# A two-layer decoder on one core: where the low weight parts of some chunks lie, how many banks a gate takes, and when the y branch's function is due

## The chip, the cores and the metric

The kernel runs on one core of a Trainium2 chip. The metric is the device time of one execution in microseconds (us). The kernel before took 1972.53 us, the median of three runs (1972.23 to 1976.43). A profile is one further execution, recorded by the hardware profiler.

## The reference, cut to what matters

One sequence of 256 positions with 2048 features goes through two layers, all in float32.

- Layer 0, recurrent block: `h = rms_norm(x)`, `y, xb = split(h @ w_in)` (2048 to 2 x 2048), a causal convolution over four positions on `xb`, then two block-diagonal gates (8 blocks of 256 x 256 each), `r = sigmoid(...)` and `i = sigmoid(...)`, a linear recurrence over the positions, and `x += (hs * gelu(y)) @ w_out`.
- Layer 1, attention: keys and values of 4 heads from `x`, queries of 32 heads, a sliding window of 128 with a sink, and `x += out @ w_o`.
- After each of them a feed-forward part: `x += (silu(gate) * up) @ w_out`, 2048 to 2 x 5632 and 5632 back to 2048.

```python
y_branch, x_branch = jnp.split(h @ w_in, 2, axis=-1)
xb = causal_depthwise_conv(x_branch, conv_w, conv_b)
hs = rg_lru(xb, w_rg, b_rg, w_ig, b_ig, lam)
return x + (hs * jax.nn.gelu(y_branch)) @ w_out
```

## The kernel before

**Split products.** TensorE multiplies in a float32 format that keeps fewer bits (float32r). So each number is split into a high part and a low part, and a product of two numbers becomes three: high by high, high by low, low by high. `split` (lines 359 to 369) makes the two parts of a chunk of weights: ScalarE (ACT) copies `raw` to `hi`, VectorE (DVE) subtracts to get `lo`.

**Chunks.** All weights stream from memory through four buffers, in chunks of 128 x 1024 floats (512 KB). Each chunk is a job, appended to `self.jobs` as a triple: where it comes from, the function that multiplies, and a third entry that says how it is split. `stream` (line 390) goes through the jobs: it loads the chunk four jobs ahead, splits the chunk three jobs ahead and calls the multiplying function of the current one. A chunk holds two blocks of 128 input features by 512 output features, so a plain job has 2 x 4 x 3 = 24 products of 128 x 128 by 128 x 256.

**Order of the products.** In `group` (line 420) a group of four output tiles goes through all chunks of its columns. In the first and middle chunks the 16 products with the high weights come first (`a` and `b`, with the inputs' high and low part), then the 8 with the low weights (`l`). In a group's last chunk the order goes by output tile. The weights are the side that is loaded into TensorE ahead of the product (still), the inputs stream through (moving). In `fast_group` (line 588) and in parts of the attention it is the other way round.

**Places.** `raw`, `hi` and `lo` are four tiles each, then come temporaries and 37 slots `s0` to `s36` of 1024 floats. Between `s6` and `s7` lies a tile `step` of 16 floats (line 105). The slots from `s7` on ("far") hold the inputs and mixed weights, `s0` to `s6` ("near") some of the mixed weights. `hi` and `lo` have 128 floats to spare, and `parts` (line 354) says where in them a chunk begins: at 0 for some kinds of chunk, at `STEP` = 32 floats for the others.

**Fast groups.** The first feed-forward product has 22 groups per layer. Groups 0 to 3 are plain ones that start before the norm is known (`start`). The even ones from 4 to 20 use a Strassen-like scheme with seven products for eight (`fast_group`, with `mix` for the weights), in seven of their eight chunks (`PAIRS`). Chunks 0 and 4 (`EVEN`) keep their mixed weights in far slots and multiply those first. The odd groups from 5 to 21 are direct ones, with weights at 0; in group 21 the last two chunks have their weights at 32 floats. The results of a fast group are transposed by `turn` (line 781), which is held back until `flush` in a later chunk.

**The recurrent block.** `ORDER` (line 54) is the order of its jobs: four x groups, four y groups of eight chunks, and eight gates of one chunk each, mostly in pairs ahead of a y group. A gate (`gates`, line 916) multiplies two input tiles by four blocks into four banks of PSUM, and four sigmoids of 128 x 256 take them out. A y group ends with four pulls (`scaled`), and its function (`y_group`, line 978: a square, a tanh, the product with the recurrence's result) is a background task that is first due six half chunks later. The results, the `z`, are the inputs of `lru_out`.

**What sets the order.** Banks are handed out from a queue: whoever frees a bank puts it at the end. Background tasks are generators; `run_bg` steps those that are due while a count of the two engines' work stays below a limit, and `yield n` puts a task off by `n` half chunks. Behind that a planner reorders the instructions of each engine by their readiness and their place in the program.

Of the kernel before, what the change touches and what calls it, by code (L numbers as in the profile page):

```python
# [49 lines left out]
class Trunk:  # L50
# [11 lines left out]
    DEBT = 2500.0  # L62
    STEP = 32
    PLAIN = 4
# [289 lines left out]
    def parts(self, i):  # L354

        o = 0 if self.jobs[i][2] is not None else self.STEP
        return (q[i % 4][:, o:o + 1024] for q in (self.hi, self.lo))

    def split(self, i):
        raw = self.raw[i % 4]  # L360
        hi, lo = self.parts(i)
        if self.jobs[i][2]:
            self.mix(i, raw, hi, lo)
            return
        n = 512 if i == 0 else 1024
        for c in range(0, 1024, n):
            q = slice(c, c + n)
            self.nc.scalar.activation(hi[:, q], raw[:, q], AF.Copy)  # L368
            self.nc.vector.tensor_tensor(lo[:, q], raw[:, q], hi[:, q].bitcast(F32), ALU.subtract)  # L369

    def mix(self, i, raw, hi, lo):

        act, tt = self.nc.scalar.activation, self.nc.vector.tensor_tensor
        d = self.double(F32, True)
        near = self.jobs[i][2] == 1
        mh, ml = self.double(near=near), self.double(near=near)
        two = lambda ap: ap.rearrange("p (a c) -> p a c", c=T)
        q = slice(T, 4 * T)
        act(hi[:, q], raw[:, q], AF.Copy)  # L379
        tt(two(d[:, 0:2 * T]), two(raw[:, T:3 * T]), raw[:, 0:T].unsqueeze(1).to_broadcast([P, 2, T]), ALU.subtract)  # L380
        tt(d[:, 2 * T:3 * T], raw[:, 2 * T:3 * T], d[:, 0:T], ALU.add)
        tt(d[:, 3 * T:4 * T], raw[:, 3 * T:4 * T], d[:, 2 * T:3 * T], ALU.subtract)  # L382
        act(mh[:, :], d[:, :], AF.Copy)  # L383
        tt(lo[:, q], raw[:, q], hi[:, q].bitcast(F32), ALU.subtract)  # L384
        self.mark = tt(ml[:, :], d[:, :], mh[:, :].bitcast(F32), ALU.subtract)  # L385
        self.free(d)
        self.mixed[i] = (mh, ml)
        self.dve += self.MORE
# [30 lines left out]

    def group(self, src, nk, xs, done, last=False, four=False, pre=None, base=0):  # L420

# [3 lines left out]
        for c in range(nk // 2):  # L425
            def mm(hi, lo, c=c):
# [18 lines left out]
                if c == nk // 2 - 1:  # L445
                    done(st["ps"])
            self.jobs.append((src(c), mm, 0 if c < base else None))

# [98 lines left out]
    def by_turns(self, w, xs, gains, r):  # L547
# [4 lines left out]
        def job(g, c):  # L552
            def mm(hi, lo):
# [16 lines left out]
                if c == last:  # L570
                    self.residual(g, ps, gains, r, part=g)
            self.jobs.append((w[g, c], mm, None))

# [5 lines left out]
    def project(self, w, nk, xs, gains, r, out=None, turns=False):  # L579
        if turns:  # L580
            self.by_turns(w, xs, gains, r)
        for g in range(2 * turns, 4):
            def done(ps, g=g):
                self.residual(g, ps, gains, r, out)
            self.group(lambda c, g=g: w[g, c], nk, xs, done, g == 3)


    def fast_group(self, src, xn, mx, g, done, final):
# [49 lines left out]
        for c in range(8):  # L638
            def mm(hi, lo, c=c):
# [5 lines left out]
                if c == 7:  # L645
                    done(st["ps"])
            self.jobs.append((src(c), mm, (c in self.PAIRS) + (c in self.EVEN)))

# [5 lines left out]
    def ffn(self, l, xs, r, gains, rn, col, out=None):  # L654
# [68 lines left out]
        for g in range(NH // 2):  # L723
# [72 lines left out]
            if g < self.PLAIN:  # L796
                self.group(src, ND, xs, start, g == self.PLAIN - 1, True)
            elif g in self.FAST:
                self.fast_group(src, xn, mx, g, joined, g == self.FAST[-1])
            else:  # L800
                end = g == self.FAST[-1] + 1
                self.group(src, ND, xn, direct, g == NH // 2 - 1, True, 6 if end else None, 6 if end else 8)
            if g == 0:
# [64 lines left out]
    def lru(self, gains, rn):  # L868
# [47 lines left out]
        def gates(n):  # L916

            def mm(hi, lo):
                x2 = [self.need(xb[2 * n + kt]) for kt in range(2)]
                ps = [self.bank() for _ in range(4)]  # L920
                for j in range(4):
                    if j == 2:
                        self.half_tick()
                    for kt in range(2):
                        c = ((j // 2) * 2 + kt) * 256 + (j % 2) * P
                        for high, q in ((1, 0), (1, T), (0, 0)):
                            nc.tensor.matmul(ps[j][:, 0:T], (hi if high else lo)[:, c:c + P], x2[kt][:, q:q + T],
                                             start=kt == 0 and high > q, stop=kt == 1 and not high)
                v = []
                for j in range(4):  # L930
                    o = self.slot(F32)
                    col = (C_BR, C_BI)[j // 2] + 2 * n + j % 2
                    self.a(o[:, 0:T], ps[j][:, 0:T], AF.Sigmoid, bias=par[:, col:col + 1])
                    self.free_bank(ps[j])
                    v.append(o)
                for kt in range(2):
                    self.free(x2[kt])
                both.extend([(2 * n, v[0], v[2]), (2 * n + 1, v[1], v[3])])
                if n % 2:
                    self.spawn(recur(list(both)))  # L940
                    both.clear()
            self.jobs.append((self.d["gate"][n], mm, None))

# [34 lines left out]
        def y_group(g):  # L978
            def done(ps):
# [6 lines left out]
                def task():  # L986
                    yield 6
                    th = []
# [38 lines left out]
    def kv(self, xs, r, gains):  # L1027
# [66 lines left out]
        for c in range(8):  # L1094
            def mm(hi, lo, c=c):
# [40 lines left out]
                if c == 7:  # L1136
                    done(ps)
            self.jobs.append((w[c], mm, None))

    def attn(self, xs, r, gains, rn):  # L1140
# [163 lines left out]
        def queries(g, c):  # L1304
            st = self.qst

            def mm(hi, lo):
# [15 lines left out]
                if c == 7:  # L1323
                    self.spawn(finish(g, st[g]))
            self.jobs.append((w[g, c], mm, 0))

# [102 lines left out]
```

## Time and profile before

| | |
|---|---|
| median of three runs | 1972.53 us |
| the profiled execution: time, span | 1969.53 us, 1967.4 us |
| TensorE busy, matmuls | 1961.1 us, 16752 |
| VectorE (DVE) busy | 1523.4 us |
| ScalarE (ACT) busy | 1128.6 us |
| read from memory | 376.06 MB |

The span goes from the first instruction to the last, the time of the execution has some 2 us more around it. A busy TensorE says only that some product was under way: products overlap, each is listed with some 277 ns, and the distance from one start to the next is what counts. A view by stretches gives the busy time and the number of matmuls that lie in a stretch; a timeline lists instructions in order of their start.

Rough places in the span: the recurrent block's x, y and gates to 209 us, `lru_out` to about 296 us, the first feed-forward part to 1010 us (its second product from about 755 us on), keys, values and attention to 1213 us with `w_o`'s first half, then its second half, and the second feed-forward part from about 1236 us to the end (its second product from about 1719 us on).

### The profile page before, as it was taken

How to read it: one execution, taken by the hardware profiler on the slowest of the kernel's cores; microseconds unless marked ns; L12 is line 12 of the kernel's file. 1: busy time of each engine (PE TensorE's matmuls, PEld its weight loads, DVE VectorE, ACT ScalarE, POOL GpSimd, SP SyncE). 2: the span in 40 equal slices, each digit the busy share in tenths (PEclk: the TensorE clock that was granted, in tenths of full speed). 3: DMA queues.
4: the chain of work that ended last, by engine and by line, in shares of the span. 5: the costliest groups of instructions: out<-in, count | busy, mean ns of one | idle time of the engine just before them, and what ended most of it. 6: DMA issues, size and time to landing. Idle time of an engine off the chain costs nothing.

```text
span 1967.4 us, 40634 instructions
## 1 busy us (share of the span) xinstructions
PE 1961.1 (100%) x16752; PEld 1933.4 (98%) x16752; DVE 1523.4 (77%) x2425; ACT 1128.6 (57%) x1620; POOL 0.2 (0%) x4
## 2 busy tenths in 40 slices
PE   9999999999999999999999999999999999999999
PEld 9999999999999999999998889999999999999999
DVE  7988868999999997544667777698999998954443
ACT  7798746555556565434556766565555555743332
POOL 0000000000000000000000000000000000000000
PEclk9999999999999999999999999999999999999999
DMA  8555665566655667555554335656556565666663
GB/s 282 182 187 182 221 216 193 187 201 212 209 199 193 206 203 245 184 186 189 185 181 158 121 129 178 212 192 204 202 195 205 194 216 198 233 207 204 204 204 128
DMA packets 107321, 384.98 MB, mean 196 GB/s; under 512 B 11904, under 2 KB 14080, under 8 KB 107136
## 3 DMA queue, kind: packets, MB, share of 16 engines
q1 hardware_dynamic: 106848, 381.99, 58.7%
q8 instruction: 131, 2.15, 0.4%
q10 hardware_dynamic: 288, 0.40, 0.1%
q14 instruction: 54, 0.44, 0.1%
HBM read 376.06 MB, written 6.29 MB: 194 GB/s over the span
## 4 chain that ended last, share of the span: by engine, by line
PE 97%; DVE 1%; ACT 1%; issue 0%; DVEq 0%; ACTq 0%
PE b L416 67%; PE b L595 18%; PE b L1316 5%; PE b L567 2%; PE b L1167 1%; DVE lo L369 1%; PE b L1231 1%; PE b L1212 1%; PE b L1122 1%; ACT s L134 0%; DVE s L147 0%; PE b L785 0%; ACT hi L368 0%; PE b L1290 0%; PE b L1356 0%
## 5 line engine op out<-in xcount | busy, mean ns | idle before, releaser
L416 PE MATMUL b<-s,hi 128*128 128x256 f32 x7936 | 1026.6, 277 | 1.3 <-ACT s L134 1.3
L416 PEld LDWEIGHTS b<-s,hi 128*128 128x128 f32 x7936 | 968.8, 188 | 2.7 <-ACT s L134 1.9
L369 DVE TENSOR_TENSOR lo<-raw,hi 128x1024 fp32r<-128x1024 f32 (+1 forms) x579 | 702.3, 1219 | 338.4 <-ACT hi L368 332.9
L368 ACT ACTIVATE hi<-raw 128x1024 fp32r<-128x1024 f32 (+1 forms) x579 | 608.4, 1056 | 491.5 <-PE b L416 435.9
L416 PE MATMUL b<-s,lo 128*128 128x256 f32 x3968 | 588.4, 277 | 0.0
L416 PEld LDWEIGHTS b<-s,lo 128*128 128x128 f32 x3968 | 514.3, 188 | 0.0
L383 ACT ACTIVATE s<-s 128x1024 fp32r<-128x1024 f32 x126 | 131.6, 1057 | 170.2 <-DVE s L382 170.2
L595 PE MATMUL b<-s,s 128*128 128x256 f32 x1512 | 195.9, 279 | 0.0
L595 PEld LDWEIGHTS b<-s,s 128*128 128x128 f32 x1512 | 183.0, 189 | 0.0
L595 PE MATMUL b<-hi,s 128*128 128x256 f32 x1044 | 178.0, 277 | 0.0
L385 DVE TENSOR_TENSOR s<-s,s 128x1024 fp32r<-128x1024 f32 x126 | 153.6, 1219 | 5.9 <-ACT s L383 5.9
L595 PEld LDWEIGHTS b<-hi,s 128*128 128x128 f32 x1044 | 152.3, 188 | 0.0
L595 PE MATMUL b<-lo,s 128*128 128x256 f32 x522 | 132.5, 276 | 0.0
L380 DVE TENSOR_TENSOR s<-raw 128x512 f32<-128x512 f32 x126 | 86.4, 686 | 41.5 <-DMA raw<-in_ffn_in 41.4
L384 DVE TENSOR_TENSOR lo<-raw,hi 128x768 fp32r<-128x768 f32 x126 | 118.4, 950 | 0.0
L134 ACT ACTIVATE s<-s 128x512 fp32r<-128x512 f32 (+3 forms) x177 | 87.2, 522 | 50.7 <-DVE s L143 34.5
L379 ACT ACTIVATE hi<-raw 128x768 fp32r<-128x768 f32 x126 | 103.0, 834 | 14.6 <-ACT s L383 7.1
L595 PEld LDWEIGHTS b<-lo,s 128*128 128x128 f32 x522 | 92.6, 188 | 0.0
L1316 PE MATMUL b<-hi,s 128*128 128x512 f32 x256 | 83.9, 408 | 0.0
L143 DVE TENSOR_TENSOR s<-s,s 128x512 fp32r<-128x512 f32 (+2 forms) x143 | 74.5, 552 | 2.2 <-ACT s L134 2.2
L134 ACT ACTIVATE s<-b 128x256 fp32r<-128x256 f32 (+4 forms) x134 | 58.6, 469 | 25.6 <-PE b L1290 5.7
L143 DVE TENSOR_TENSOR s<-b,s 128x512 f32<-128x512 f32 (+3 forms) x126 | 63.6, 531 | 3.8 <-ACT s L134 2.6
(115 smaller groups left out, 1171.5 us busy)
## 6 DMA issues: line engine op xcount, KB each, us to landing
raw<-in_ffn_in SPq DMA_DIRECT2D x352, 512.0 KB, 3.4
raw<-in_ffn_out SPq DMA_DIRECT2D x176, 512.0 KB, 3.7
raw<-in_lru_in SPq DMA_DIRECT2D x63, 512.0 KB, 4.2
raw<-in_lru_out SPq DMA_DIRECT2D x32, 512.0 KB, 4.3
raw<-in_w_q SPq DMA_DIRECT2D x32, 512.0 KB, 3.3
raw<-in_w_o SPq DMA_DIRECT2D x32, 512.0 KB, 3.4
raw<-in_gate SPq DMA_DIRECT2D x8, 512.0 KB, 4.2
away<-s SPq DMA_DIRECT2D x8, 512.0 KB, 4.0
```

The source lines that it names most:

```text
L134: self.nc.scalar.activation(out, in_, func, **kw)
L143: self.nc.vector.tensor_tensor(out, a, b, op)
L368: self.nc.scalar.activation(hi[:, q], raw[:, q], AF.Copy)
L369: self.nc.vector.tensor_tensor(lo[:, q], raw[:, q], hi[:, q].bitcast(F32), ALU.subtract)
L379: act(hi[:, q], raw[:, q], AF.Copy)
L380: tt(two(d[:, 0:2 * T]), two(raw[:, T:3 * T]), raw[:, 0:T].unsqueeze(1).to_broadcast([P, 2, T]), ALU.subtract)
L383: act(mh[:, :], d[:, :], AF.Copy)
L384: tt(lo[:, q], raw[:, q], hi[:, q].bitcast(F32), ALU.subtract)
L385: self.mark = tt(ml[:, :], d[:, :], mh[:, :].bitcast(F32), ALU.subtract)
L416: self.nc.tensor.matmul(ps[f][:, 0:T], w, x2[k][:, c0:c1], start=f not in begun, stop=last and all(q[1] != f for q in todo[n + 1:]))
L595: nc.tensor.matmul(st["ps"][b][:, h % 2 * T:(h % 2 + n) * T], x, w, start=b not in st["begun"], stop=True, skip_group_check=True)
L1316: nc.tensor.matmul(st[g][b][:, :], x, q, start=c + kt == 0 and x is xh and q is wh, stop=c == 7 and kt == 1 and q is wl)
```

## The change

Three edits.

1. The third entry of a job becomes a pair of offsets, one for `hi` and one for `lo` (a triple for mixed chunks). A new kind of chunk, `LEVEL_W`, has its high parts at 32 floats as before and its low parts at 16 floats. It is used for chunk 1 of the plain groups 1 and 3 of the feed-forward part, of all four groups of each second feed-forward product, of the four groups of `lru_out` and of the last two groups of `w_o`, and for chunk 6 of the last direct group (group 21). The other kinds keep their offsets.
2. A gate takes two banks instead of four: two of its tiles lie side by side in a bank. Only the first product into a bank starts a new sum there. The two banks are freed after the last of the four sigmoids.
3. The y branch's function is first due four half chunks after its group, not six.

```diff
-    STEP = 32
+    PLAIN_W, LEVEL_W, PLAIN_X, MIXED, MIXED_FAR = (32, 32), (32, 16), (0, 0), (0, 0, 1), (0, 0, 2)
+    LEVEL = (1,)
...
     def parts(self, i):
 
-        o = 0 if self.jobs[i][2] is not None else self.STEP
-        return (q[i % 4][:, o:o + 1024] for q in (self.hi, self.lo))
+        at = self.jobs[i][2]
+        return (q[i % 4][:, o:o + 1024] for q, o in zip((self.hi, self.lo), at))
...
-    def group(self, src, nk, xs, done, last=False, four=False, pre=None, base=0):
+    def group(self, src, nk, xs, done, last=False, four=False, pre=None, base=0, level=()):
...
-            self.jobs.append((src(c), mm, 0 if c < base else None))
+            self.jobs.append((src(c), mm, self.PLAIN_X if c < base else self.LEVEL_W if c in level else self.PLAIN_W))
...
-            self.group(lambda c, g=g: w[g, c], nk, xs, done, g == 3)
+            self.group(lambda c, g=g: w[g, c], nk, xs, done, g == 3, level=self.LEVEL)
...
-                self.group(src, ND, xs, start, g == self.PLAIN - 1, True)
+                self.group(src, ND, xs, start, g == self.PLAIN - 1, True, level=self.LEVEL if g % 2 else ())
...
-                self.group(src, ND, xn, direct, g == NH // 2 - 1, True, 6 if end else None, 6 if end else 8)
+                self.group(src, ND, xn, direct, g == NH // 2 - 1, True, 6 if end else None, 6 if end else 8, (6,))
...
-                ps = [self.bank() for _ in range(4)]
+                ps = [self.bank() for _ in range(2)]
+                cut = lambda j: ps[j // 2][:, j % 2 * T:j % 2 * T + T]
...
-                            nc.tensor.matmul(ps[j][:, 0:T], (hi if high else lo)[:, c:c + P], x2[kt][:, q:q + T],
-                                             start=kt == 0 and high > q, stop=kt == 1 and not high)
+                            nc.tensor.matmul(cut(j), (hi if high else lo)[:, c:c + P], x2[kt][:, q:q + T],
+                                             start=j % 2 + kt == 0 and high > q, stop=True, skip_group_check=True)
...
-                    self.a(o[:, 0:T], ps[j][:, 0:T], AF.Sigmoid, bias=par[:, col:col + 1])
-                    self.free_bank(ps[j])
+                    self.a(o[:, 0:T], cut(j), AF.Sigmoid, bias=par[:, col:col + 1])
                     v.append(o)
+                for p in ps:
+                    self.free_bank(p)
...
-                    yield 6
+                    yield 4
```

The remaining lines of the diff only rewrite the third entry of the other jobs (`None` to `PLAIN_W`, `0` to `PLAIN_X`, the mixed kinds to `MIXED` and `MIXED_FAR`).

More of the change, by code (lines that the diff above doesn't have):

```diff
@@ L361, in split @@
         hi, lo = self.parts(i)
-        if self.jobs[i][2]:
+        if len(self.jobs[i][2]) > 2:
             self.mix(i, raw, hi, lo)
@@ L374, in mix @@
         d = self.double(F32, True)
-        near = self.jobs[i][2] == 1
+        near = self.jobs[i][2] is self.MIXED
         mh, ml = self.double(near=near), self.double(near=near)
@@ L571, in mm @@
                     self.residual(g, ps, gains, r, part=g)
-            self.jobs.append((w[g, c], mm, None))
+            self.jobs.append((w[g, c], mm, self.PLAIN_W))
         for q in (range(last - 1), range(last - 1, last + 1)):
@@ L646, in mm @@
                     done(st["ps"])
-            self.jobs.append((src(c), mm, (c in self.PAIRS) + (c in self.EVEN)))
+            kind = self.PLAIN_X if c not in self.PAIRS else self.MIXED_FAR if c in self.EVEN else self.MIXED
+            self.jobs.append((src(c), mm, kind))
     def flush(self):
@@ L941, in mm @@
                     both.clear()
-            self.jobs.append((self.d["gate"][n], mm, None))
+            self.jobs.append((self.d["gate"][n], mm, self.PLAIN_W))
         both = []
@@ L1137, in mm @@
                     done(ps)
-            self.jobs.append((w[c], mm, None))
+            self.jobs.append((w[c], mm, self.PLAIN_W))
     def attn(self, xs, r, gains, rn):
@@ L1324, in mm @@
                     self.spawn(finish(g, st[g]))
-            self.jobs.append((w[g, c], mm, 0))
+            self.jobs.append((w[g, c], mm, self.PLAIN_X))
         self.qst = {}
```

## The prediction

> **What bounds the kernel now.** I read the page first, then the matmul rows by stretch of time, then short timelines of the three places the change touches.
>
> ```profile
> span 1967.4 us, 40634 instructions
> PE 1961.1 (100%) x16752; PEld 1933.4 (98%) x16752; DVE 1523.4 (77%) x2425; ACT 1128.6 (57%) x1620; POOL 0.2 (0%) x4
> PEclk9999999999999999999999999999999999999999
> PE 97%; DVE 1%; ACT 1%; issue 0%; DVEq 0%; ACTq 0%
> ```
>
> TensorE has work all the time, at full granted clock, and it is 97% of the chain that ended last. So the time is the number of matmuls times the pitch from one start to the next, plus the few waits. "Busy" cannot show the pitch; a count over a stretch can. The next rows are stretch, length, busy (count):
>
> ```profile
> 212.00:296.00 84.00, 84.00 (x743) 1.00 0.68 221
> 755.00:1005.00 250.00, 250.00 (x2125) 1.00 0.58 190
> 1722.00:1960.00 238.00, 238.00 (x2102) 1.00 0.60 193
> 395.87:754.05 358.18, 358.18 (x3150) 1.00 0.62 208
> 1360.64:1718.82 358.18, 358.18 (x3150) 1.00 0.62 207
> ```
>
> Rows two and three are the same code, `ffn_out` of layer 0 and of layer 1: 250/2125 = 117.65 ns a matmul against 238/2102 = 113.23 ns. Row one (`lru_out`) has 84/743 = 113.1. There is thus a **fast pitch, 113.2**, and a **slow pitch, 117.65**, 4.42 ns apart, at the same clock and the same positions of the data; a whole stage stays in the one or the other. Where does it fall in? Both stages begin behind the four transposes of the last `turn`:
>
> ```profile
> 754.18 0.60 PE L785 MATMUL b<-con,s 128*128 128x128 f32 x4
> 754.53 0.36 PE L416 MATMUL b<-s,hi 128*128 128x256 f32 x1
> 1718.94 0.60 PE L785 MATMUL b<-con,s 128*128 128x128 f32 x4
> 1719.30 0.37 PE L416 MATMUL b<-s,hi 128*128 128x256 f32 x1
> ```
>
> The same instructions with the same 0.35 us from the transposes to the first product, once into the slow pitch and once into the fast one. I read it as two states in which the weight load for the next product and the running product can follow each other: which one is taken is decided by the last disturbance, and nothing in an undisturbed stage changes it.
>
> **Part 1, the low parts of 20 chunks.** From `raw` on, every tile of the constant pool is a multiple of 512 bytes except `step`, 16 floats, which lies ahead of the slots s7 to s36 that hold the inputs. So inputs lie at 64 bytes past a multiple, weights of a plain chunk at 32 floats = 128, the changed low parts at 16 floats = 64. The distance, moving side minus still side, is 64 - 128 = -64 in a plain chunk; it goes to 0 for the eight low products of one chunk, and back. The trace has distance 0 already, in the mixed chunks 0 and 4 of each fast group, where the mixed weights lie in far slots like the inputs:
>
> ```profile
> 384.02 0.28 PE L416 MATMUL b<-s,lo 128*128 128x256 f32 x1
> 384.13 1.60 PE L595 MATMUL b<-s,s 128*128 128x256 f32 x12
> 385.57 0.40 PE L595 MATMUL b<-hi,s 128*128 128x256 f32 x2
> 385.81 0.28 PE L595 MATMUL b<-lo,s 128*128 128x256 f32 x1
> 385.93 0.39 PE L595 MATMUL b<-hi,s 128*128 128x256 f32 x2
> 386.16 0.28 PE L595 MATMUL b<-lo,s 128*128 128x256 f32 x1
> 386.27 0.39 PE L595 MATMUL b<-hi,s 128*128 128x256 f32 x2
> ```
>
> Price: twelve level products take 385.57 - 384.13 = 1.44 us, 120.0 ns each; the next three take 0.36 us, still 120, and the three after that 0.34 us, 113.3. A level run of eight thus costs 8 x 6.8 + 3 x 6.8 = 75 ns. They are 2 plain groups, 1 last direct group and 4 `ffn_out` groups per layer, 4 `lru_out` groups and 2 groups of `w_o`: 20, so **+1.5 us** (only 0.4 us if all were entered slow, 8 x 2.35 ns each).
>
> What it does to the state: behind a level run of a fast group the weights move at 0 and the inputs stand at 64, so the distance is -64, that of the plain chunks too. There are 9 fast groups x 2 level runs in each layer. The two 358.18 us rows hold 16 full runs of 12, 3150 matmuls of which 32 are transposes (four in 0.35 us). 3118 x 113.3 ns = 353.3 us, the level runs 16 x 15 x 6.8 ns = 1.6, the transposes 8 x 0.35 = 2.8: 357.7. The 0.5 us that is left would pay for 110 slow products in all, fewer than stand between two level runs, although half of the runs come right behind four transposes, the kind of disturbance that made 754.53 slow. So a level run seems to put the two streams into one fixed relation, from which distance -64 is left fast. **The sum takes that**: of the 2160 products from 754.53 on, the 16 high ones of chunk 6 stay slow, the eight low ones are level, and 24 + 4 x 22 x 24 = 2136 become fast: 2136 x 4.42 ns = **-9.4 us**. Bounds: 0 if the state survives; the loss side is the second rival.
>
> [...]
>
> **Part 2, a gate's four tiles in two banks.** Same 24 products, same four sigmoids, half the banks. Now the rows around the gates:
>
> ```profile
> 100.00:200.00 100.00, 98.06 (x843) 1.00 0.56 181
> 128.48 0.38 PE L416 MATMUL b<-s,hi 128*128 128x256 f32 x1 [0.21 <-ACT s L134]
> 154.21 0.36 PE L927 MATMUL b<-s,hi 128*128 128x256 f32 x1 [0.54 <-DVE h L143]
> 158.03 0.38 PE L416 MATMUL b<-s,hi 128*128 128x256 f32 x1 [0.75 <-ACT s L134]
> 186.70 0.39 PE L416 MATMUL b<-s,hi 128*128 128x256 f32 x1 [0.37 <-ACT s L134]
> 127.95 0.84 ACT L134 ACTIVATE s<-b,par 128x256 f32<-128x256 f32 x2
> 153.39 0.28 PE L927 MATMUL b<-s,lo 128*128 128x256 f32 x1
> 153.65 1.08 DVE L143 TENSOR_TENSOR h<-b,rstd 128x256 f32<-128x256 f32 x3
> 154.97 0.42 DVE L143 TENSOR_TENSOR h<-b,rstd 128x256 f32<-128x256 f32 x1
> 154.09 1.14 ACT L134 ACTIVATE s<-h 128x256 f32<-128x256 f32 x3 [3.23 <-DVE h L143]
> ```
>
> 843 matmuls at 113.3 ns are 95.5 us of the 100: **4.5 us** of waits. The rows show whose: each y group begins in the banks of the first of the two gates ahead of it and waits for that gate's sigmoids (ACT), and the second gate of a pair begins in the banks of the y group that has just ended and waits for its pulls (DVE). With two banks a gate, both gates of a pair fit into the four banks that are free, and the next y group gets the banks of the y group before it. Those pulls end at 154.97 + 0.42 = 155.39, while y2 could start behind the pair's second gate, 24 products, at 153.39 + 0.11 + 24 x 0.1133 = 156.2 at the earliest: the wait goes.
>
> What is late next: the two engines that fed those banks.
>
> ```profile
> 131.00:150.00 19.00, 19.00 (x170) 19.00 (x170) 15.77 (x29) 18.95 (x38) 0.00 (x0) 1.00 0.52 168
> 160.00:180.00 20.00, 20.00 (x179) 20.00 (x178) 16.92 (x31) 19.95 (x40) 0.00 (x0) 1.00 0.56 172
> 200.00:230.00 30.00, 30.00 (x267) 30.00 (x267) 29.56 (x58) 22.78 (x40) 0.00 (x0) 1.00 0.61 194
> 225.94 0.75 DVE L143 TENSOR_TENSOR s<-s,s 128x256 fp32r<-128x256 f32 x2
> 228.03 0.39 PE L416 MATMUL b<-s,hi 128*128 128x256 f32 x2
> 228.37 0.39 PE L416 MATMUL b<-s,hi 128*128 128x256 f32 x2
> ```
>
> Columns four and five are DVE and ACT: ACT has 0.1 us to spare in 39 us behind the gates, DVE 0.4 us in the 30 us in which `lru_out` begins. The last two z of y3 are ready at 226.69, and TensorE asks at 228.03 + 0.11 for the first of them and at 228.49 for the second: 1.8 us to spare. With TensorE 4.5 us ahead, up to 2.7 us of it is handed back there or at a late weight split.
>
> **Part 3, y's function due two half chunks earlier.** No instruction is added or removed. A half chunk is 12 products, 1.36 us, so its steps are due 2.7 us earlier: the same size as what part 2 would hand back, for y3's z if the planner follows. Behind its steps on DVE and ACT stand the weight splits and the recurrence. The trace cannot show the new order. Together, parts 2 and 3 give between -4.5 us and +1.3 us (nothing won, and one more table load, 1.28 us, on the full ACT):
>
> ```profile
> 126.66 1.28 ACT L134 ACT_TABLE_LOAD   x1
> ```
>
> I take **-3.0 us**: all 4.5, less about half of the 2.7.
>
> **Sum.** The profiled execution took 1969.53 us (span 1967.4 and 2.1 around it). 1969.53 - 9.4 + 1.5 - 3.0 = 1958.6. The median of the runs, 1972.53, is 3.0 us above it, as much as some 680 more products at the slow pitch would cost; most places where those could lie have a level chunk now, the first 200 us have none. I add 0.4: **1959.0 us**.
>
> **Rivals.**
>
> *The level chunks change nothing (or only toss the coin anew).* For: no run at -64 that was slow is seen to turn fast through a level run; those in the trace come behind fast products or transposes. Against: the identical ends of all of them. Time: 1969.53 + 0 to 1.5 - 3.0 = 1966.5 to 1968, on the runs' scale up to 1971. [...]
>
> *Slower: a level chunk leaves the slow state behind it.* In the fast groups it is the moving side that steps from level to -64; in the change it is the still side, so the first high product after the level run could lock the other way. The place is that product, and it decides from the first group. Products that follow a level chunk and are fast now: `lru_out` about 740, plain groups 550 and 770, `w_o` 360, `ffn_out` of layer 1 2112, the end of its direct group 24: 4556 x 4.42 = 20.1 us. Level runs entered slow cost 0.4. 1969.53 + 20.1 + 0.4 - 3.0 = 1987.0. Against it: only the difference of the two positions has shown any effect so far.
>
> *The gates' waits only move.* ACT and DVE are full, and TensorE meets late weight splits or a late z instead. 1969.53 - 9.4 + 1.5 + (0 to 1.3) = 1961.6 to 1962.9. For it: the 18.95 of 19 and 29.56 of 30; against it: ACT stands idle for 3.23 us before 154.09, until the pulls come, so not all of the stage is full.
>
> **How the numbers follow.** Forecast 0.60 (1955 to 1962), waits only move 0.18, level chunks do nothing 0.13, slower 0.09. The range 1953 to 1970 holds the first two and most of the third: the low end is the whole 4.5 with 1 us beside, the high end the third rival with most of the 3.0. What a measurement can tell from no change is about 0.2%, 3.9 us: faster means below 1968.6. Forecast, moved waits and a part of the third case are faster, the rest of that case the same: 0.82, 0.09, 0.09.
>
> **What would show it.** Right: over 755 to 1005 us (a few us earlier) about 2205 matmuls in 250 us, not 2125; eight products at 120 ns and then 113.3 in chunk 1 of each `ffn_out` group; in 100 to 200 us above 870 matmuls, no wait of a first y product on a sigmoid. Wrong: a stage that is slow behind a level run (first or second rival); waits of the matmuls on L368, L369 or the z tiles between 130 and 230 us (third rival); more table loads on ACT there.

## The result, and the profile after

The changed kernel takes 1995.57 us (median), the kernel before, on the same chip, 1972.39: a ratio of 1.0117, with a 95% interval of 1.0102 to 1.0132. It is 23 us slower; the forecast was 1959.0. One of its six runs took 3013.94 us at a granted clock of 0.607 and is left out. The profiled execution took 1994.93 us. Its page begins:

```profile
span 1992.9 us, 40635 instructions
PE 1982.4 (99%) x16752; PEld 1955.1 (98%) x16752; DVE 1525.1 (77%) x2425; ACT 1139.5 (57%) x1626; POOL 0.2 (0%) x4
```

The matmuls are the same 16752, the span is 25.5 us longer. ACT has six instructions more and is busy 10.9 us longer, DVE and the rest are as they were. Matmuls by stretch, after (stretch, length, then busy time and count of PE, of its weight loads, of DVE, ACT and POOL, then the granted clock of TensorE, the share of DMA, GB/s):

```profile
212.00:296.00 84.00, 81.58 (x677) 80.97 (x677) 61.34 (x102) 47.23 (x74) 0.00 (x0) 0.98 0.63 206
395.00:755.00 360.00, 360.00 (x3165) 360.00 (x3164) 328.22 (x455) 209.56 (x251) 0.00 (x0) 1.00 0.61 204
755.00:1005.00 250.00, 250.00 (x2129) 250.00 (x2128) 140.30 (x165) 116.08 (x142) 0.00 (x0) 1.00 0.59 194
1722.00:1960.00 238.00, 238.00 (x2027) 238.00 (x2027) 121.27 (x122) 97.91 (x101) 0.00 (x0) 1.00 0.62 201
```

`ffn_out` of layer 1 was fast, with 2102 matmuls in its 238 us, and now has 2027: 117.4 ns each. `ffn_out` of layer 0 was slow and still is (2129 in 250 us). The fast groups (395 to 755 us) have not changed. `lru_out` lost both pitch and time to waits (677 matmuls, PE idle for 2.4 of the 84 us, and a mean granted clock of 0.98, which is taken up below). The place where the pitch turns, in `ffn_out` of layer 1 (timeline: start, length, instruction, count):

```profile
1736.68 0.62 PE L417 MATMUL b<-s,hi 128*128 128x256 f32 x4
1737.14 1.12 PE L417 MATMUL b<-s,lo 128*128 128x256 f32 x8
1738.10 0.40 PE L417 MATMUL b<-s,hi 128*128 128x256 f32 x2
1738.33 0.28 PE L417 MATMUL b<-s,lo 128*128 128x256 f32 x1
1738.45 0.40 PE L417 MATMUL b<-s,hi 128*128 128x256 f32 x2
```

The eight level products take 1738.10 - 1737.14 = 0.96 us, 120 ns each, as forecast. Behind them three products take 0.35 us, 117 ns each. The four ahead took 0.46, 115 each with the step in it; the level run was entered fast and left slow. In what follows a product is called slow if it is not level and the next one starts 115.5 to 122 ns after it; counted so through the whole trace, there are 2549 before and 6843 after, and over 113.3 ns each they cost 11.6 and 30.7 us. That is **19.1 of the 25.5 us**.

Most of the rest lies between 100 and 240 us. Waits of PE there, before and after (what waited, for what; total us, times, longest), and the table loads on ACT (count; total us, mean ns; idle before):

```profile
PE b L416 <- ACT s L134: 1.3, 3, 0.8
PE b L927 <- DVE h L143: 0.5, 1, 0.5
...
L134 ACT ACT_TABLE_LOAD x14 | 18.0, 1283 | 0.2
```

```profile
PE b L417 <- ACT hi L369: 3.7, 3, 2.0
PE b L417 <- ACT s L135: 2.4, 1, 2.4
...
L135 ACT ACT_TABLE_LOAD x20 | 25.7, 1283 | 0.4
```

The waits of before are gone, as forecast, and larger ones stand in their place: on late weight splits, and in `lru_out` on a late z. Between 100 and 240 us the distances over 122 ns (from one start to the next, above 113.3 each) cost 4.5 us before and 10.9 after: **6.4 us more**. Not all of that is waiting. Behind the two longest distances, 2.2 us at 135.5 and 2.7 us at 227.8, the granted clock is 0.50 for 3.4 us, once each:

```profile
138.30:141.60 3.30, 3.30 (x18) 3.30 (x17) 2.75 (x5) 3.30 (x8) 0.00 (x0) 0.50 0.48 158
230.50:233.80 3.30, 3.30 (x14) 3.09 (x15) 3.15 (x8) 0.63 (x2) 0.00 (x0) 0.50 0.72 264
```

The starts there are some 213 ns apart, not 113. The room of 16 products at 100 ns more makes 1.6 us for each of the two places, so about half of the 6.4 us (an estimate from these rows) is the lower clock. In the kernel before the clock is 1.00 from 7 to 1966 us. It does not follow each time: a distance of 2.2 us at 136 us in e2 (below) has no lower clock behind it. Elsewhere the distances over 122 ns cost 0.9 us less than before, and the 160 level products, at 120 ns, 1.0 us more than at 113.3. 19.1 + 6.4 - 0.9 + 1.0 = 25.6, against 25.5.

### The profile page after: what moved, and what is told of

Read it like the earlier page. It is cut to its first block, busy times and chain, and to the rows that moved or that the text cites. A ratio compares the mean times of both kernels' runs of the same rounds, so it can differ in the third digit from the quotient of the medians.

```text
span 1992.9 us, 40635 instructions
## 1 busy us (share of the span) xinstructions
PE 1982.4 (99%) x16752; PEld 1955.1 (98%) x16752; DVE 1525.1 (77%) x2425; ACT 1139.5 (57%) x1626; POOL 0.2 (0%) x4
## 4 chain that ended last, share of the span: by engine, by line
PE 95%; ACT 2%; DVE 2%; issue 0%; DMA 0%; ACTq 0%; DVEq 0%
PE b L417 66%; PE b L596 18%; PE b L1320 5%; PE b L568 2%; ACT s L135 1%; PE b L1171 1%; DVE lo L370 1%; ACT hi L369 1%; PE b L1235 1%; ACT L135 1%; PE b L1216 1%; PE b L1126 1%; PE b L930 1%; DVE s L148 0%; PE b L787 0%
## 5 line engine op out<-in xcount | busy, mean ns | idle before, releaser
L417 PE MATMUL b<-s,hi 128*128 128x256 f32 x7936 | 1042.9, 279 | 6.1 <-ACT hi L369 3.7
L417 PEld LDWEIGHTS b<-s,hi 128*128 128x128 f32 x7936 | 983.7, 189 | 7.5 <-ACT hi L369 4.3
L417 PE MATMUL b<-s,lo 128*128 128x256 f32 x3968 | 595.9, 279 | 0.0
L417 PEld LDWEIGHTS b<-s,lo 128*128 128x128 f32 x3968 | 520.4, 189 | 0.0
L135 ACT ACTIVATE s<-b 128x256 fp32r<-128x256 f32 (+4 forms) x134 | 58.6, 469 | 25.6 <-PE b L1294 5.7
```

The source lines that it names most:

```text
L135: self.nc.scalar.activation(out, in_, func, **kw)
L417: self.nc.tensor.matmul(ps[f][:, 0:T], w, x2[k][:, c0:c1], start=f not in begun, stop=last and all(q[1] != f for q in todo[n + 1:]))
```

## The experiments

"Theory A" is: a level run that ends with a step of the still side leaves the slow pitch behind it. The first four kernels take the change apart.

**The level chunks alone (e1).** Against the changed kernel:

```diff
-                ps = [self.bank() for _ in range(2)]
+                ps = [self.bank() for _ in range(4)]
...
-                    yield 4
+                    yield 6
```

> The kernel before with the level chunks alone; gates and y's function as before. Theory A (a level run that ends with a step of the still side leaves the slow pitch behind it, one that ends with a step of the moving side leaves the fast pitch): the trace of the changed kernel has about 4300 slow products more than that of before, at 4.42 ns some 19 us, and 0.4 us of level products more. So about 1990 us against 1972, ratio 1.009 to 1.010; lru_out, ffn_out of layer 0 and ffn_out of layer 1 all at about 117.7 ns a matmul behind their first level run. Rival S (the slow pitch comes from the other order of the gates' stage, the level runs do nothing): 1972 to 1974 us, ffn_out of layer 1 at 113.2 ns as before. The forecast's reading (level runs leave the fast pitch): 1964 us.

1989.73 us, ratio 1.0093 (1.0077 to 1.0108). Theory A's numbers come, and rival S, in which the gates' stage is to blame, falls. `ffn_out` of layer 1, by the stretch 1735 to 1955 us, before and then here:

```profile
1735.00:1955.00 220.00, 220.00 (x1943) 220.00 (x1943) 103.65 (x93) 86.10 (x81) 0.00 (x0) 1.00 0.61 196
```

```profile
1735.00:1955.00 220.00, 220.00 (x1870) 220.00 (x1869) 104.74 (x99) 85.70 (x84) 0.00 (x0) 1.00 0.62 197
```

113.2 ns against 117.6. All 20 level runs leave the slow pitch; five of them were entered fast. Not all slow products of this profile come from level runs: 1310 of them, 5.9 us, lie before 209 us, ahead of the first level run, and waits there cost 3.2 us less than before. The chance start that does this is the subject of e4.

**Both edits of the gates' stage (e2), the banks alone (e3), the due time alone (e4).** Against the changed kernel e2 has:

```diff
-    LEVEL = (1,)
+    LEVEL = ()
...
-                self.group(src, ND, xn, direct, g == NH // 2 - 1, True, 6 if end else None, 6 if end else 8, (6,))
+                self.group(src, ND, xn, direct, g == NH // 2 - 1, True, 6 if end else None, 6 if end else 8)
```

e3 has besides:

```diff
-                    yield 4
+                    yield 6
```

and e4, instead of that, a gate's four banks as in e1:

```diff
-                ps = [self.bank() for _ in range(2)]
+                ps = [self.bank() for _ in range(4)]
```

> The kernel before with two banks a gate and y's function due after four half chunks; no level chunks. Theory A: what is left of the loss, the new waits of 100 to 240 us (6 more table loads on ACT): +5 to +6.5 us, about 1978 us, with the slow pitch only where it was before (about 755 to 1010 us). Rival S: about 1995 us, with slow stages as in the changed kernel. The forecast's reading: 1969.5 us (-3.0).

> Two banks a gate, y's function due after six half chunks as before, no level chunks. Theory D (the earlier due time puts squares and tanhs between the gates' sigmoids, which costs the table loads): 11 table loads between 120 and 225 us as before, the waits on sigmoids and pulls gone: -3 to -4.5 us, 1968 to 1969.5 us. Rival B (the banks alone do it, since the gates now come sooner and ACT is full): 15 or more table loads, +3 to +6 us, 1975 to 1978 us.

> Four banks a gate as before, y's function due after four half chunks, no level chunks. Theory D: 15 or more table loads between 120 and 225 us, +3 to +6 us, 1975 to 1978 us. Rival B: 11 to 12 table loads and -0.5 to +1 us, 1972 to 1973.5 us.

| | us | ratio | table loads, 100 to 240 us | slow products before 260 us |
|---|---|---|---|---|
| before | 1972.27 | | 14 | 53 |
| e2, both | 1976.52 | 1.0027 (1.0015 to 1.0039) | 20 | 209 |
| e3, banks | 1973.71 | 1.0004 (0.9989 to 1.0019) | 16 | 1004 |
| e4, due time | 1972.21 | 0.9999 (0.9990 to 1.0008) | 14 | 1542 |

e1 and e2 add up to the whole: 1.0093 x 1.0027 = 1.0120, against 1.0117. Within the intervals, some 3 us each, the two losses don't depend on each other. e2's profile has one stretch at half clock, 1.6 us, behind a stop of 3.2 us from one start to the next, and e3's one behind a stop of 2.2 us; e4's has none. The two halves of e2 cost nothing that can be measured by themselves, but they cannot be compared here: their first stage runs at other pitches. Stretch 60 to 120 us, before and in e4, where the edit has not yet had any effect (the first y group ends behind it):

```profile
60.00:120.00 60.00, 60.00 (x532) 60.00 (x531) 58.19 (x112) 48.92 (x78) 0.00 (x0) 1.00 0.59 188
```

```profile
60.00:120.00 60.00, 60.00 (x511) 60.00 (x511) 58.14 (x111) 48.76 (x79) 0.00 (x0) 1.00 0.58 189
```

112.8 against 117.4 ns. The order of the instructions on PE, DVE and ACT is the same in both up to here, so something other than the program decides the pitch at the very start; it is called chance here, and what it is stays open. e4 has lost nearly all of its waits (0.5 us against 4.8 between 10 and 260 us) and paid 6.9 us for slow products. Theory D (the due time alone brings the table loads) falls with e4's 14. Rival B (the banks alone do it) has the 16 loads that it expected of e3, but not the 3 to 6 us.

**More level products (e5).** Against e1:

```diff
-    PLAIN_W, LEVEL_W, PLAIN_X, MIXED, MIXED_FAR = (32, 32), (32, 16), (0, 0), (0, 0, 1), (0, 0, 2)
+    PLAIN_W, LEVEL_W, PLAIN_X, MIXED, MIXED_FAR = (32, 32), (16, 32), (0, 0), (0, 0, 1), (0, 0, 2)
```

> As e1, but in each level chunk the sixteen high products are level (still side at the inputs' position) and the eight low ones behind them stand at -64. Theory A: the still side makes the step at the end again, so the products behind each of the 20 level runs are slow again (117 to 118 ns), as in e1; a level run of sixteen at 120 ns costs little more than eight, so about 1990 to 1992 us. Rival L (length decides: eight level products are too few to bring TensorE into the fast pitch, the twelve of the fast groups are enough, so sixteen are too): fast pitch of 113.3 ns behind the level runs, ffn_out of layer 1 at 113.2 and of layer 0 at about 113.5, so 1962 to 1966 us.

1990.19 us in one run (before, beside it, 1973.42). Sixteen level products, then eight low ones, in `ffn_out` of layer 1:

```profile
1738.81 2.08 PE L417 MATMUL b<-s,hi 128*128 128x256 f32 x16
1740.73 1.11 PE L417 MATMUL b<-s,lo 128*128 128x256 f32 x8
```

(1740.73 - 1738.81)/16 = 120 ns; all 20 runs leave the slow pitch. Length is not what differs from the fast groups.

**The other sign (e6), and level runs there (e7).** The prediction counted places from `raw`, which itself lies 128 bytes past a multiple of 512. From here on they are counted whole: the inputs and level weights are at 192, plain weights at 32 floats are at 256, plain weights at 0 floats at 128. e6 is the kernel before with

```diff
-    PLAIN_W, LEVEL_W, PLAIN_X, MIXED, MIXED_FAR = (32, 32), (32, 16), (0, 0), (0, 0, 1), (0, 0, 2)
+    PLAIN_W, LEVEL_W, PLAIN_X, MIXED, MIXED_FAR = (0, 0), (32, 16), (0, 0), (0, 0, 1), (0, 0, 2)
```

and no level chunks; e7 against e1:

```diff
-    PLAIN_W, LEVEL_W, PLAIN_X, MIXED, MIXED_FAR = (32, 32), (32, 16), (0, 0), (0, 0, 1), (0, 0, 2)
+    PLAIN_W, LEVEL_W, PLAIN_X, MIXED, MIXED_FAR = (0, 0), (0, 16), (0, 0), (0, 0, 1), (0, 0, 2)
```

> The kernel before with all plain weights at 0 floats in place of 32 (the distance moving side minus still side is +64 in plain chunks, not -64); no level chunks, gates and y's function as before. In the trace of before +64 stands only in the direct groups, fast each time. Theory P (+64 has no slow pitch that holds): the 2549 slow products of before, 11.6 us, go: 1960 to 1962 us. Rival Q (which side stands higher does not matter, the last disturbance decides): ffn_out of layer 0 still at about 117.7 ns, 1970 to 1974 us. Theory A alone says nothing on +64.

> As e6, with the 20 level chunks: high parts at 0 floats (+64), eight low ones level, so the still side steps back from level to +64 at the end. If theory A holds for either sign: 117 to 118 ns behind each level run, about 1985 to 1992 us. If the sign of the step decides, or +64 has no slow pitch: 113.3 ns behind each level run, and e6's time plus 20 x 75 ns = 1.5 us.

e6: 1985.54 us, ratio 1.0065 (1.0050 to 1.0080). Rival Q is right that +64 is no fast place; theory P, with 1960 to 1962 us, falls. Neither expected more stages slow than before (6885 slow products). e7, the same with 20 level runs, took 1968.68 in one run: 17 us less than e6, and below the 1973.42 of before. Stretch 775 to 1005 us in `ffn_out` of layer 0, e6 and e7:

```profile
775.00:1005.00 230.00, 230.00 (x1955) 230.00 (x1954) 119.73 (x135) 99.68 (x119) 0.00 (x0) 1.00 0.57 189
```

```profile
775.00:1005.00 230.00, 230.00 (x2030) 230.00 (x2029) 121.35 (x133) 102.52 (x121) 0.00 (x0) 1.00 0.59 195
```

117.6 and 113.3 ns. So a level run does set the pitch, also for the better: when the still side steps **down** from level to 128, not up to 256. Theory A, in which each step of the still side leaves the slow pitch, falls with that. A run of e7 that leaves the fast pitch, and one of its two that don't:

```profile
1720.10 1.12 PE L417 MATMUL b<-s,lo 128*128 128x256 f32 x8
1721.06 0.39 PE L417 MATMUL b<-s,hi 128*128 128x256 f32 x2
1721.29 0.28 PE L417 MATMUL b<-s,lo 128*128 128x256 f32 x1
1721.40 0.39 PE L417 MATMUL b<-s,hi 128*128 128x256 f32 x2
```

```profile
762.72 1.12 PE L417 MATMUL b<-s,lo 128*128 128x256 f32 x8
763.68 0.40 PE L417 MATMUL b<-s,hi 128*128 128x256 f32 x2
763.92 0.28 PE L417 MATMUL b<-s,lo 128*128 128x256 f32 x1
764.04 0.40 PE L417 MATMUL b<-s,hi 128*128 128x256 f32 x2
```

Three products take 0.34 us in the first, 0.36 in the second, which came to its level run slow.

**Is it the side or the direction? (e12)** In the fast groups it is the moving side that steps, and it steps down (192 to 128). This kernel is the one before with that step turned upward. To that end the plain parts of all mixed chunks start at 32 floats, so within a fast group the moving side also goes from 256 to 128 and back, without a level run between:

```diff
-    PLAIN_W, LEVEL_W, PLAIN_X, MIXED, MIXED_FAR = (32, 32), (32, 16), (0, 0), (0, 0, 1), (0, 0, 2)
+    PLAIN_W, LEVEL_W, PLAIN_X, MIXED, MIXED_FAR = (32, 32), (32, 16), (0, 0), (32, 32, 1), (32, 32, 2)
```

> The kernel before; only in the mixed chunks of the fast groups the plain parts of the weights, there the moving side, start at 32 floats in place of 0. Behind the 36 level runs the moving side then steps up from level (192 to 256 bytes past a multiple of 512), not down (192 to 128), and stays there for 18 products. Theory U (up leaves the slow pitch, down the fast one, whichever side steps): these 18 at about 117.7 ns, 36 x 18 x 4.4 ns = 2.9 us at least, and up to 25 us where the slow pitch then holds through the rest of the fast groups: 1975 to 1997 us. Theory W (a step of the moving side always leaves the fast pitch, only the still side's depends on its direction): 113.3 ns there and 1970 to 1974 us.

1987.95 us in one run (before, beside it, 1969.36). Theory U: all 36 level runs, behind which the kernel before is fast each time, leave the slow pitch, and it holds through the rest of each fast group:

```profile
395.00:755.00 360.00, 360.00 (x3059) 360.00 (x3058) 320.29 (x439) 205.10 (x243) 0.00 (x0) 1.00 0.61 199
...
526.38 1.67 PE L596 MATMUL b<-s,s 128*128 128x256 f32 x12
...
528.24 0.40 PE L596 MATMUL b<-hi,s 128*128 128x256 f32 x2
...
528.60 0.40 PE L596 MATMUL b<-hi,s 128*128 128x256 f32 x2
```

3059 matmuls where the changed kernel has 3165. The fourth to sixth product behind the twelve level ones take 0.36 us, where the prediction's rows for the kernel before have 0.34. The first level run of each layer is entered fast in both kernels and behind the same instructions, so what decides is the step behind it. Up leaves the slow pitch and down the fast one, on either side. In all these kernels up ends at 256 bytes and down at 128: whether it is the direction of the step or the place where it ends is not told apart. A step from 256 to 128 without a level run does not bring the fast pitch back (360/3059 is 117.7 ns). The place without a level run ahead of it does not decide, as e6 with its weights at 128 has more slow stages than the kernel before with 256 (6885 slow products against 2549).

**With +64, the due time once more (e8).** Against e6:

```diff
-                    yield 6
+                    yield 4
```

> As e6, and y's function due after four half chunks; four banks a gate. In the profile of e4 the waits of the gates' stage were gone (0.5 us against 4.8) and what they had cost went into slow products (1542 of them before 260 us, 6.9 us). Theory P: no slow products, so both gains hold: e6 less 4 to 4.5 us, 1956 to 1958 us. Rival Q: as e4, 1970 to 1974 us.

1984.29 us, ratio 1.0057 (1.0041 to 1.0074), 1.25 us from e6 and far above both expectations, 1956 to 1958 and 1970 to 1974. With 7107 slow products it says little on the due time: TensorE is later, and the waits of e6 and e8 between 10 and 260 us are 2.3 and 0.6 us, against 4.8 before.

**The gates' stage at the fast pitch (e9, e10, e11, e13).** e9 is e7 with level chunks in the first stage too:

```diff
-            self.group(lambda c: w[4 + g, c], ND, xs, done)
+            self.group(lambda c: w[4 + g, c], ND, xs, done, level=self.LEVEL)
...
-            self.group(lambda c: w[g, c], ND, xs, done, g == 3)
+            self.group(lambda c: w[g, c], ND, xs, done, g == 3, level=self.LEVEL)
```

e10 has the edit of e8 besides, e13 a gate's two banks as in the changed kernel, e11 both.

> e7 (plain weights at 0 floats, low parts of the level chunks at 16, gates and y's function as before), with chunk 1 of the eight x and y groups level as well. Theory A2 (the step of the still side decides: up to a higher address leaves the slow pitch, down leaves the fast one; e1, e5: 40 steps up, all slow; e7: 20 steps down, 18 fast): the slow products before 260 us, 1702 in e7 at 7.6 us, fall below 400; the waits there, 2.3 us, come back to 4 to 5 since TensorE is ahead again; eight level runs cost 0.6 us. 1968.7 - 6 + 2 + 0.6 = 1965 us, between 1961 and 1967. If the steps decide nothing and e7's fast stages were luck: 1968 to 1985 us.

> As e9, and y's function due after four half chunks, four banks a gate. In a stage that is fast before and after, the due time alone can be seen: by e4's profile (waits 0.5 us before 260 us, 14 table loads between 100 and 240 us as in the kernel before) e9 less 3 to 4 us, about 1961 us. Rival: with TensorE at the fast pitch the waits only move to the weight splits, e9 +-1 us.

> As e10, and a gate's four tiles in two banks. Theory G (two banks let y's function and the next gates' sigmoids run into each other, 6 more table loads and the waits on splits and z, 10.7 us of waits in e2 against 4.8 before and 0.5 in e4): e9 +5 to +6 us and e10 +8 to +10, about 1970 us. Rival (e2's loss came from its chance start, not from the two edits): within 2 us of e10.

> As e9, a gate's four tiles in two banks, y's function due after six half chunks. Theory G2 (only both edits together bring y's function among the gates' sigmoids; e3 has 16 table loads between 100 and 240 us against 14 before and 20 in e2 and e11): 14 to 16 table loads, e9 -1 to +2 us, 1962.5 to 1965.5 us. Theory B (the banks alone cost it, the due time nothing): 20 table loads, 1969 to 1971 us.

| | us | ratio to before | table loads, 100 to 240 us | first square root of the first recurrence | sigmoids of the next pair from |
|---|---|---|---|---|---|
| e9, neither | 1963.51 | 0.9970 (0.9959 to 0.9982) | 14 | 145.47 us | 157.22 us |
| e10, due time | 1963.70 | 0.9967 (0.9956 to 0.9979) | 14 | 149.58 | 156.18 |
| e13, banks | 1962.79 | 0.9951 (0.9937 to 0.9964) | 16 | 151.01 | 157.24 |
| e11, both | 1970.70 | 0.9999 (0.9990 to 1.0009) | 20 | 153.84 | 158.12 |

(The kernel before had a median of 1969.36 us beside e9 to e11 and 1972.23 beside e13; the ratios differ by that.) Each edit is free, both together cost 7 us: theory G2. (e10 was expected 3 to 4 us below e9; the rival, within 1 us of it, came.) The spans of e10 and e11 are 7.9 us apart: 5.0 us of that are distances over 122 ns, with one stretch at half clock (1.6 us) among them, and 3.1 us are more slow products. The last two columns show where it begins. ACT in e10, then in e11, behind the first pair's sigmoids (`s<-b,par`); the exponentials and tanhs of the recurrence are `s<-s,cc`:

```profile
127.81 1.57 ACT L135 ACTIVATE s<-b,par 128x256 f32<-128x256 f32 x4
129.26 1.08 ACT L369 ACTIVATE hi<-raw 128x1024 fp32r<-128x1024 f32 x1
130.21 1.59 ACT L135 ACTIVATE s<-b,par 128x256 f32<-128x256 f32 x4
131.81 1.28 ACT L135 ACT_TABLE_LOAD   x1
```

```profile
130.03 0.85 ACT L135 ACTIVATE s<-b,par 128x256 f32<-128x256 f32 x2
130.90 1.28 ACT L135 ACT_TABLE_LOAD   x1
132.20 0.51 ACT L135 ACTIVATE s<-s,cc 128x256 f32<-128x256 f32 x1
132.72 1.28 ACT L135 ACT_TABLE_LOAD   x1
134.02 0.84 ACT L135 ACTIVATE s<-b,par 128x256 f32<-128x256 f32 x2
134.75 0.51 ACT L135 ACTIVATE s<-s,cc 128x256 f32<-128x256 f32 x1
135.27 1.28 ACT L135 ACT_TABLE_LOAD   x1
136.57 0.51 ACT L135 ACTIVATE s<-s,cc 128x256 f32<-128x256 f32 x1
```

With two banks, an exponential was set ahead of the third sigmoid of the second gate, and that costs two table loads more than in e10, 1.28 us each. e13 has these two as well. Why the planner sets it there is not shown. On the chip that sigmoid had nothing to wait for: the last product of the gate starts at 128.23 us in e13, the first of the two loads at 130.83. The due time puts y's steps on DVE ahead of the recurrence's: the last four of the recurrence's steps that feed the square roots (`s<-s`) begin at 139.35 us in e9 and at 147.72 in e10. The last one of them in e9, in e10 and in e11:

```profile
146.78 0.76 DVE L148 SCALAR_TENSOR_TENSOR s<-s 128x256 f32<-128x256 f32 x2
```

```profile
147.72 1.43 DVE L148 SCALAR_TENSOR_TENSOR s<-s 128x256 f32<-128x256 f32 x4
```

```profile
157.37 0.42 DVE L148 SCALAR_TENSOR_TENSOR s<-s 128x256 f32<-128x256 f32 x1
```

It starts at 147.12, 148.73 and 157.37 us, and at 152.92 in e13; the next pair's sigmoids come 10.1, 7.5 and 0.8 us later, 4.3 in e13. Either delay alone fits into the time between the square roots and the next pair's sigmoids: 11.8 us in e9, 6.6 in e10, 6.2 in e13. With both it is 4.3, and the last square root falls among the sigmoids, with two loads more; the same happens at the third pair:

```profile
158.12 1.57 ACT L135 ACTIVATE s<-b,par 128x256 f32<-128x256 f32 x4
159.71 1.28 ACT L135 ACT_TABLE_LOAD   x1
161.01 0.42 ACT L135 ACTIVATE s<-s 128x256 f32<-128x256 f32 x1
...
162.39 1.28 ACT L135 ACT_TABLE_LOAD   x1
163.69 1.57 ACT L135 ACTIVATE s<-b,par 128x256 f32<-128x256 f32 x4
```

Which of these functions has a load ahead of it is read here from the rows, with the program's order (the exponential of a tile comes ahead of its tanh): at 134.75 us the tanh follows the sigmoids without a load, the exponential at 136.57 has one of 1.28 us ahead of it, and the square root at 161.01 has one of 1.28 us on either side. The order on ACT is what the rows show; that e13's two loads are hidden because that slack is left, and e11's six are not because it is gone, is read from the table and was not tried by itself.

**Fewer level chunks, placed by the rule (e14).** e9 with level chunks only behind places that leave the slow pitch:

```diff
-            self.group(lambda c, g=g: w[g, c], nk, xs, done, g == 3, level=self.LEVEL)
+            self.group(lambda c, g=g: w[g, c], nk, xs, done, g == 3, level=(0, 2) if g == 2 * turns else ())
...
-                self.group(src, ND, xs, start, g == self.PLAIN - 1, True, level=self.LEVEL if g % 2 else ())
+                self.group(src, ND, xs, start, g == self.PLAIN - 1, True, level=() if g else (0, 5))
...
-            self.group(lambda c: w[4 + g, c], ND, xs, done, level=self.LEVEL)
+            self.group(lambda c: w[4 + g, c], ND, xs, done, level=((1,), (1,), (0,), ())[g])
...
-            self.group(lambda c: w[g, c], ND, xs, done, g == 3, level=self.LEVEL)
+            self.group(lambda c: w[g, c], ND, xs, done, g == 3, level=(0,))
```

The direct groups have none.

> As e9, with level chunks only behind places that leave the slow pitch: chunk 1 of x0 and x1, chunk 0 of x2 and of each y group, chunks 0 and 5 of the first plain group, chunks 0 and 2 of the first group of lru_out, of both ffn_out and of the last part of w_o. Where a stage is fast it stays fast without more of them: 15 level runs for 28 save 1.0 us, and the earlier places some 300 slow products, 1.3 us: e9 -1 to -2.5 us, 1961 to 1962.5 us. If the fast pitch has to be renewed in each group, ffn_out falls back to 117.7 ns somewhere: 1968 us or more.

1962.73 us, ratio 0.9951 (0.9940 to 0.9963): 0.5% faster than the kernel before and 1.65% faster than the changed one by the two medians (1962.73 / 1995.57), though no better than e13 beside it and just above the 1961 to 1962.5 expected. (It has 19 level runs; the expectation counted 15.) One group of `ffn_out` sets the pitch for all four; 1735 to 1955 us:

```profile
1735.00:1955.00 220.00, 220.00 (x1944) 220.00 (x1943) 100.35 (x92) 82.84 (x78) 0.00 (x0) 1.00 0.59 188
```

Level runs, by the step that ends them (by the pitch two places ahead and six or more behind; where four transposes stand right ahead, as at 16 of the 36 runs of e12 and of before, this is counted as fast):

| step at the end | entered fast, left fast | fast, slow | slow, fast | slow, slow |
|---|---|---|---|---|
| still side up (after, e1, e5) | 0 | 14 | 0 | 46 |
| still side down (e7, e9, e10, e11, e13, e14) | 92 | 0 | 47 | 12 |
| moving side up (e12) | 0 | 18 | 0 | 18 |
| moving side down (before) | 36 | 0 | 0 | 0 |

The runs of the fast groups in the other fourteen kernels, 36 in each, end with the moving side down as well. All of them were left fast, ten of them (two each in after, e1, e5, e6 and e8) though they were entered slow.

## Why the prediction was wrong, step by step

- **What bounds the kernel: right.** Two pitches at one clock, kept through whole stages, are in every trace above, at 113.2 to 113.3 and 117.6 ns. That they are two ways in which the weight load and the running product follow each other was the author's reading; no run shows it. The stretches at half clock behind long waits, two in the changed kernel, were not foreseen.
- **Part 1, the price of a level run: right.** 120 ns a product. Since 16 of the 20 runs were entered slow, they cost some 0.5 us against the pitch ahead of them, near the 0.4 given for that case, not 1.5.
- **Part 1, the state behind it: wrong, and this is the step that failed.** "a level run seems to put the two streams into one fixed relation, from which distance -64 is left fast", on which the -9.4 us rested, was drawn from 36 runs in which the moving side steps down; the change has the still side step up. The prediction saw that difference and gave it 0.09, "only the difference of the two positions has shown any effect so far". That sentence had nothing to stand on: the level runs of the kernel before all ended with the same step of the same side, so its trace could not show an effect of either. The second rival gave 20.1 us for the slow products, and 19.1 were counted. Without its -3.0 for the gates it came to 20.5 us more than before, and e1, which has no other edit, took 17.5 us more by the medians (1989.73 against 1972.27). That its 1990.0 us is so near 1989.73 is in part luck: it counts from the profiled 1969.53.
- **Part 2 and part 3, -3.0 us: wrong in sign.** The waits it named did go, and the engine it named as late next was late next. What failed is the size: the upper bound of "+1.3 us (nothing won, and one more table load, 1.28 us, on the full ACT)". Six loads came, 7.7 us on an engine that had 0.1 us to spare in 39, and e2 measures +5.3 us, of which its stretch at half clock is 1.6. The prediction treated the three moves as one pool of 4.5 us to be shared out. By e10 and e13 each edit alone is free, and by e11 the pair is not: what the two use up is the time between the square roots and the next sigmoids, which the prediction did not look at.
- **The first rival** (the level chunks change nothing): its lower end, 1966.5, takes level products at no cost. No run shows that; the 160 of the changed kernel took 120 ns each, 1.0 us more in all than at 113.3.
- **The third rival** (the waits only move) named the place but had the level chunks gain 9.4.
- **The range:** its low end, 1953, doesn't follow from the words given for it. The whole 4.5 us and 1 us beside give 1955 to 1956.
- **What would show it:** the reading of `ffn_out` behind a level run and of the waits on the splits, set down as signs of the rivals, decided it at once.

**What stays open.** Why the step decides, and whether its direction counts or the place where it ends. When a long wait is followed by the half clock. Why 12 of the 59 downward runs that were entered slow were left slow too. What a stop of TensorE or the four transposes leave behind: `ffn_out` of layer 0 begins slow and that of layer 1 fast in before and in e6. Why the planner splits the second gate's sigmoids. And why at +64 without level runs more stages are slow.

## What to carry to other kernels

A rule drawn from a trace holds for the cases that are in the trace: list what all of them have in common (here the side that steps and its direction) and count whatever the change does otherwise as unknown, at even odds. Where a TensorE-bound stage shows two pitches at one clock, count matmuls by stretch and look at how the operands' addresses step ahead of it; a few products in another place can turn thousands (in e14 eight level ones set the pitch of the 2000 behind them). Look at the granted clock behind each long wait before all of the loss is put down to waiting. And two edits that each use up the same slack on a full engine are priced together, not one by one.

## What the runs showed of the hardware that was not expected

- Products of 128 x 128 by 128 x 256 had three pitches in these traces, by where the two operands lie relative to each other: 120.0 ns where both lie the same distance past a multiple of 512 bytes, and 113.3 or 117.6 ns at 64 bytes apart. Other distances were not looked at. Which of these two comes was set by a step from level and then held, in e14 for the 2000 products of an `ffn_out` behind its second level run. It also differed from one kernel to the next where the program was the same (112.8 ns before and 117.4 in e4, from 60 to 120 us), and changed behind transposes (in the kernel before, 113.3 ns for the 24 products from 748.73 to 751.45 us and 117.65 from 755 us on, with the four at 754.18 between).
- Stepping from level to 64 bytes higher left the slow pitch 96 times in 96, on either side; stepping to 64 bytes lower left the fast one 175 times in 187, and each time it was entered fast or right behind transposes. The distance between the two is no guide: -64 was left slow by the still side's step up and fast by the moving side's step down.
- In four traces a stop of TensorE, 2.2 to 3.2 us from one start to the next, is followed by 3.4 us at a granted clock of 0.50 (after, twice; e2, e3 and e11, once each), with products some 213 ns apart. e2's other stop, of 2.2 us, is not.
- The pitch of the first 50 to 190 us is not set by the program alone: 532 or 511 products in the same 60 us of the same code. That is up to 7 us between two kernels (0.2 us of slow products before 260 us in the kernel before, 6.9 in e4), more than the 5.3 us that e2 measures for the edits of that stage.
